# A hybrid decoder step on one core: a new order of the mixer's work, and two more engines run in order of emission

## The chip, the cores and the metric

The kernel runs on one core of one Trainium2 chip. The metric is the device time of one execution in microseconds (us). TensorE (PE, with its weight loads shown apart as PEld), VectorE (DVE), ScalarE (ACT), GpSimd (POOL) and SyncE (SP, which issues transfers) each work through their own list of instructions and wait for each other by semaphores.

## What is computed

Two layers of a decoder, for a prompt of 256 tokens and 8 samples of 4 new tokens, carried together as 288 columns of a transposed activation. Each layer is: x + half a SwiGLU FFN, then a mixer with three parallel branches, then another half FFN.

```python
def _trunk(x, pos, ret_s, hg_s, lru_h, conv_buf, p):
    for l in range(DEPTH):
        x = x + 0.5 * _swiglu(_rmsnorm(x, p['ffn1_norm'][l]), p['ffn1_w_gate'][l], p['ffn1_w_up'][l], p['ffn1_w_down'][l])
        m, st = _mixer(_rmsnorm(x, p['mix_norm'][l]), pos, l, ret_s[l], hg_s[l], lru_h[l], conv_buf[l], p)
        x = x + m.astype(x.dtype)
        x = x + 0.5 * _swiglu(_rmsnorm(x, p['ffn2_norm'][l]), p['ffn2_w_gate'][l], p['ffn2_w_up'][l], p['ffn2_w_down'][l])
```

The mixer projects the normed input by one wide matrix into queries, keys, values and gates, runs 4 retention heads (width 128 by 256), 8 HGRN2 heads (128 by 128) and an RG-LRU over 8 blocks of 128 channels (convolution, two sigmoid gates, a scan), norms and gates each branch, projects it, and merges the three by sigmoid gates. The new states of all heads are outputs too. d_model is 1024, the FFN's hidden width 2816.

## The kernel before, in words

**Units.** Every large matrix product is cut into units: one unit multiplies a 1024-row, 128-column piece of weights with the activations into a 128 by 288 block. The kernel works in fp32 accuracy with the faster fp32r format: weights are split into a high part `wh` (a copy by ACT, line 127 through `act`) and a low part `wl` (a subtraction by DVE, L231), activations likewise (`chunk` pairs), and `gemm` (L245 to L247) issues 8 x 3 = 24 matmuls per unit: high x high, high x low, low x high. A layer has 44 units of gate and up weights and 24 shorter ones of down weights in each FFN, and 128 units in the mixer.

**Weights.** SP loads 512 KB pieces into five buffers `wr`. `next_w` keeps the splits ahead: when unit n begins, the split of unit n + 2 is emitted (`LOOK = 2`); there are three `wh`/`wl` pairs, so that this split waits until the matmuls of unit n - 1 are done.

**Order of the mixer.** `PLAN` is a list of items, written out by hand: `Rn` and `Hn` are the projections of retention head n (four units) and of HGRN2 head n (three), `Xn` is an input block of the RG-LRU, `GLn`, `GHn`, `GRn` are output gates, `T0n` to `T2n` merge gates, `OLn`, `OHn`, `ORn` output projections, `OMn` the last projection. The rest of the work (the heads themselves, the gates and scans of the RG-LRU, the norms) is written as generators. `pump()` is called after almost every unit and runs one step of every generator without weight, and as many steps of heads as a credit allows (`RATE` is added per pump, up to `CAP`). A head is started with a weight, and the active weights may add up to `MAXACT = 2`: an HGRN2 head weighs 1, a retention head 2, so that it runs alone. Where a unit needs a head that is not done, `until` pumps until it is; `do_h` and `do_r` pump until no head is queued. `norm_later` collects the squares of finished heads, and norms four of them at a time (`NORMS`; Ln and Exp on ACT, each with another table than its neighbours).

**Order on the engines.** `tc.manual_schedule(engines={PE})` (L112) makes the order of emission the order of TensorE's instructions. For the other engines the framework's scheduler chooses an order, with `evac()` as a priority for what empties a PSUM bank. An engine then always works through its list in that order.

**Start of a norm.** A unit's matmuls run on activations that are scaled by the gain but not by 1/rms; the rms comes from `norm_rstd` (a matmul with ones, L284, a square root on ACT, a reciprocal on DVE, L279) after the first unit, and results are multiplied by it. In the mixer the first `NXG = 4` units are done so; meanwhile `renorm` (L445, L483) makes properly normed `chunk` pairs for the others.

**RG-LRU.** `lru_scan` handles four blocks at once: one step has eight exponentials and tanhs and four squares on ACT, a later one four square roots, the next ones the scans on DVE.

**States.** `st` has three buffers of 512 KB. A retention head takes two, an HGRN2 head one; POOL's queue loads them, SP's writes them out when the head is done. A head's first step splits the loaded state (`split_s`, ACT `sh`, DVE `sl`).

**Constants.** The tables for masks and rotary angles are loaded through POOL's queue as the program begins. `derived` (three steps on ACT, with another table each) computes gate constants during the first FFN.

Of the kernel before, what the change touches and what calls it, by code (L numbers as in the profile page):

```python
# [19 lines left out]
P = 128  # L20
# [16 lines left out]
LS = 3 + TP  # L37

WB = 12
NORMS = 4  # L40
LRU = (range(0, 4), range(4, 8))
MAXACT = 2
RATE = 1.65
CAP = 2.5
LOOK = 2
NRAW = 5
HEAD = 4
NXG = 4
EVAC = 100
DOWN = ((0, 8), (8, 15), (15, 22))  # L50
LEVELS = (1, 2, 4, 8, 16, 32, 64)
# [8 lines left out]


PLAN = (
# [4 lines left out]
).split()  # L67


def units_of(item):  # L70
    kind, n = item[:-1], int(item[-1])
    if kind == "H":
        return [("in", C_FH + n), ("in", C_QH + n), ("in", C_IH + n)]
    if kind == "R":
        return [("in", C_QR + n), ("in", C_KR + n), ("in", C_VR + 2 * n), ("in", C_VR + 2 * n + 1)]
    base = {"X": C_XL, "GL": C_GL, "GH": C_GH, "GR": C_GR,
            "T0": C_GATE, "T1": C_GATE + 8, "T2": C_GATE + 16}
    if kind in base:
        return [("in", base[kind] + n)]
    return [({"OL": "lru", "OH": "hgrn", "OR": "ret", "OM": "mix"}[kind], n)]  # L80
# [21 lines left out]
def tile_hybrid(ctx: ExitStack, tc, i, o):  # L102
# [6 lines left out]
    pacc = ctx.enter_context(tc.tile_pool(name="pacc", bufs=3, space=PSUM))  # L109
    pmix = ctx.enter_context(tc.tile_pool(name="pmix", bufs=5, space=PSUM))  # L110

    ctx.enter_context(tc.manual_schedule(engines={mybir.EngineType.PE}))  # L112

    sets = {AF.Sigmoid: 2, AF.Sqrt: 3, AF.Exp: 0, AF.Ln: 5, AF.Silu: 18, AF.Gelu_apprx_tanh: 11, AF.Tanh: 0}
    groups = {"set": None, "cur": [], "prev": []}
# [41 lines left out]
    par = cp.tile([P, NPAR], F32, name="par")  # L157

    scratch = cp.tile([P, 1], F32, name="scratch")

    def ready(func):
        act(scratch, onec, func)
# [2 lines left out]

    def const(name, shape, dt=F32):
        t = cp.tile(list(shape), dt, name="c_" + name)
        nc.gpsimd.dma_start(t, i[name])
        consts[name] = t
        return t  # L170

    ones = cp.tile([P, P], F32, name="ones")
    nc.vector.memset(ones, 1.0)
# [143 lines left out]
    def ffn(l, which, nx, next_norm):  # L317
        xh, xl, ss = nx
        hh, hl = chunks(F32R, NF), chunks(F32R, NF)
        for m in range(NF):  # L320
            pg, pu = accps(), accps()
            for u, ps in ((0, pg), (1, pu)):
                wh, wl = next_w()
                gemm(ps[:, :T], wh, wl, NC, xh, xl, 0, True, True)
                if m == 0 and u == 0:
                    rstd = norm_rstd(ss)
            with evac():
                zg = small([P, T], tag="z", bufs=4)
                tt(zg, pg[:, :T], rstd, ALU.mult)  # L329
                act(zg, zg, AF.Silu)  # L330
                zu = small([P, T], tag="z", bufs=4)
                tt(zu, pu[:, :T], rstd, ALU.mult)  # L332
                tt(zu, zu, zg, ALU.mult)  # L333
                hi, lo = hh[m], hl[m]
                act(hi, zu, AF.Copy)
                tt(lo, zu, hi.bitcast(F32), ALU.subtract)
            pump()
        ny = next_norm()
        ready(AF.Sqrt)
        for m in range(NC):  # L340
            ps = accps()
            for k0, k1 in DOWN:
                wh, wl = next_w()
                for kk in range(k0, k1):
                    a, b, j = hh[kk], hl[kk], kk - k0
                    mm(ps[:, :T], wh[:, j, :], a, start=kk == 0, stop=False)  # L346
                    mm(ps[:, :T], wh[:, j, :], b, start=False, stop=False)  # L347
                    mm(ps[:, :T], wl[:, j, :], a, start=False, stop=kk == NF - 1)  # L348
            with evac():
                stt(x[:, m, :], ps[:, :T], 0.5, x[:, m, :], op0=ALU.mult, op1=ALU.add)  # L350
                next_post(m, ny)
            pump()
        return ny
# [2 lines left out]
    active, queue, done = [], [], set()  # L356

    def start(gen, weight):
        if weight:
            queue.append([gen, weight])  # L360
        else:
            active.append([gen, 0])

    credit = [0.0]

# [17 lines left out]

    def norm_later(sq, scale, scaled):
        later.append((sq, scale, scaled))
        if len(later) == NORMS:
            norms_now()

    def norms_now():
        if later:  # L390
# [37 lines left out]
    def mixer(l, nx):  # L428
# [58 lines left out]

        xx, xcw, xc, rr, ii, aa = {}, {}, {}, {}, {}, {}
        h0 = small([P, NC, NB], tag="h0", bufs=1)
        nc.gpsimd.dma_start(h0, i["state_lru"][l])  # L490
        cv0 = small([P, NC, NB, 3], tag="cv0", bufs=1)
        nc.gpsimd.dma_start(cv0, i["state_conv"][l])
        cr = small([P, T], tag="cr", bufs=1)
        sr = small([P, T], tag="sr", bufs=1)
        nc.gpsimd.dma_start(cr, i["cosc"])
        nc.gpsimd.dma_start(sr, i["sinc"])
        cvo = small([P, NC, 1 + NB, 3], tag="cvo", bufs=1)
        def lru_in(n):
            xx[n], xcw[n], rr[n], ii[n] = chunks(F32, 4, LP)
            xc[n], aa[n], rr[n], ii[n] = (a[:, :LY] for a in (xcw[n], xx[n], rr[n], ii[n]))  # L500
            xn, xcn = xx[n], xc[n]
            xs = seqs(xn[:, LS:])
            lw = small([P, 2, P], tag="lw")
            nc.gpsimd.dma_start(lw, i["lru_w"][l, n])
            nc.gpsimd.memset(xn[:, 0:3], 0.0)
            nc.gpsimd.tensor_copy(xs[:, :, 0:3], cv0[:, n])
            ps = unit_in(C_XL + n)
            psv = ps[:, TP:].rearrange("p (b t) -> p b t", t=DS)
            with evac():
                if normed():  # L510
                    act(xn[:, 3 : 3 + P], ps[:, :P], AF.Copy)
                    act(xn[:, 3 + P : LS], ps[:, P:TP][:, ::-1], AF.Copy)
                    act(xs[:, :, 3:7], psv, AF.Copy)
                else:
                    tt(xn[:, 3 : 3 + P], ps[:, :P], src["r"][:, :P], ALU.mult)
                    tt(xn[:, 3 + P : LS], ps[:, P:TP][:, ::-1], src["r"][:, P:TP][:, ::-1], ALU.mult)
                    tt(xs[:, :, 3:7], psv, src["r"][:, TP:].rearrange("p (b t) -> p b t", t=DS), ALU.mult)
            nc.gpsimd.tensor_copy(cvo[:, n, 0, :], xn[:, TP:LS])
            nc.gpsimd.tensor_copy(cvo[:, n, 1:, :], xs[:, :, 4:7])
            cw = PARAMS["conv_w", l]  # L520
            act(xcn, xn[:, 0:LY], AF.Identity, scale=par[:, cw + n : cw + n + 1], bias=pcol("conv_b", l, n))
            for t in range(1, 4):
                stt(xcn, xn[:, t : t + LY], par[:, cw + 8 * t + n : cw + 8 * t + n + 1], xcn,
                    op0=ALU.mult, op1=ALU.add)
            start(lru_gates(n, lw), weight=0)
            pump()
# [99 lines left out]
        def pairs(a, off, d):  # L626
            return free(a, TP + off, (DS, NB), (1, DS - d))

        def hgrn_head(h, f, k, q, qt, zv, zr):
            st = small([P, NB, P], tag="st", bufs=3)  # L630
            nc.gpsimd.dma_start(st, i["state_hgrn"][l, h])
            pr = small([P, PR], tag="pr", bufs=2)
            tt(pr[:, :T], k, q, ALU.mult)
            lev = []
# [27 lines left out]
            for d in range(1, DS):  # L662
                w = NB * (DS - d)
                po = PR_S[d]
                tt(pr[:, po : po + w].rearrange("p (b t) -> p b t", b=NB), pairs(k, 0, d), pairs(qt, d, d), ALU.mult)
                tt(pairs(qt, d, d), pairs(qt, d, d), pairs(f, 0, d), ALU.mult)
            kc = scale(0)
            qm = sample_q(qt[:, TP:])
            sp = split_s(st)
# [170 lines left out]
        def ret_head(h, q, k, kr, vv, v1):  # L840
            sts = []
            for j in range(2):
                st = small([P, NB, P], tag="st", bufs=3)
                nc.gpsimd.dma_start(st, i["state_ret"][l, h, j])
                sts.append(st)
            dm = small([P, 3 * P], tag="dm", bufs=1)
            nc.gpsimd.dma_start(dm, i["dmask"][h])
            qd = small([P, TS], tag="qd")
            tt(qd, q[:, TP:], qdec[:, h, :], ALU.mult)
            qm = sample_q(qd)  # L850
# [73 lines left out]
        def do_r(h):  # L924
            q = rotary(C_QR + h)
            pump()
            k = rotary(C_KR + h)
            kr = replicate(k)
            pump()
            while queue:  # L930
                pump()
            vv = [vtiles() for _ in range(2)]
            v1 = small([96, 2, P], F32R, tag="v1r", bufs=2)
            for j in range(2):
                zv = zsb(C_VR + 2 * h + j)
                zr = replicate(zv)
                start(ret_v(zv, zr, *vv[j], v1[:, j, :]), weight=0)
                pump()
            start(ret_head(h, q, k, kr, vv, v1), weight=2)

        def ret_v(zv, zr, vT, vs, v1):
            yield
# [55 lines left out]

        run["X"] = do_x
        for item in PLAN:  # L1000
            run[item[:-1]](int(item[-1]))
            if item[0] not in "HRX":
                pump()
# [146 lines left out]
```

## Time and profile before

| | |
|---|---|
| median of 3 runs | 1921.11 us (1916.91 to 1921.69) |
| the profiled execution, its own time | 1919.22 us |
| its span, first to last instruction | 1917.1 us |
| TensorE busy | 97% of the span |
| VectorE, ScalarE busy | 71%, 57% |
| table loads on ScalarE | 86, 110.3 us in all |
| layer 1: FFN, mixer, FFN | from 5.7, from 227.3, from 755.6 us |
| layer 2: FFN, mixer, FFN | from about 965, from 1173.8, from 1702 us |

The span is the time of the instructions; the run's own time is 2.1 us longer, and stands 0.1% below the median. A busy time counts overlapping instructions once; matmuls are pipelined, so that a matmul's own duration (about 0.3 us) is more than twice the distance between two.

### The profile page before, as it was taken

The numbers are of one execution on the slowest core, as the hardware profiler recorded it, in microseconds if no ns is written. First come the engines' busy times: TensorE is split into PE (matmuls) and PEld (weight loads), VectorE is DVE, ScalarE is ACT, GpSimd is POOL, SyncE is SP. The second block draws the span as 40 slices with busy tenths as digits, with TensorE's granted clock in tenths as the row PEclk, the third lists the DMA queues.
The fourth block names the chain that finished last, engine by engine and source line by source line (L and its number), as shares of the span: only waits on it lengthen the run. The fifth ranks groups of instructions, "written<-read, shape, count | busy, mean of one in ns | idle before, by whom it ended". The sixth has DMA issues, their size and how long they took to land.

```text
span 1917.1 us, 36198 instructions
## 1 busy us (share of the span) xinstructions
PE 1860.3 (97%) x14040; PEld 1832.0 (96%) x14040; DVE 1363.4 (71%) x2756; ACT 1098.2 (57%) x2005; POOL 96.0 (5%) x252
## 2 busy tenths in 40 slices
PE   7999999999999989999999999999999999999998
PEld 7999989999899989999999999999999999999997
DVE  6665688877788767665566657888877986676654
ACT  6444478656666665444444444886657656654443
POOL 2000013100000000000000000220000000000000
PEclk9999999999999999999999999999999999999999
DMA  7555545545555555555555554556455554455553
GB/s 248 174 170 159 164 129 181 174 159 187 185 185 157 158 163 163 169 168 157 174 165 167 163 169 141 153 162 213 146 187 183 162 169 139 150 165 166 165 161 95
DMA packets 94843, 318.41 MB, mean 166 GB/s; under 512 B 11248, under 2 KB 17312, under 8 KB 94672
## 3 DMA queue, kind: packets, MB, share of 16 engines
q1 hardware_dynamic: 87552, 293.74, 50.0%
q0 software_dynamic: 6544, 21.77, 3.4%
q8 instruction: 111, 1.82, 0.4%
q10 hardware_dynamic: 576, 0.59, 0.1%
q14 instruction: 60, 0.49, 0.1%
HBM read 295.71 MB, written 20.35 MB: 165 GB/s over the span
## 4 chain that ended last, share of the span: by engine, by line
PE 83%; DVE 8%; ACT 6%; issue 2%; DMA 1%; SPq 0%; POOL 0%; DVEq 0%; POOLq 0%; ACTq 0%
PE acc L245 20%; PE acc L246 20%; PE acc L247 20%; PE acc L347 5%; PE acc L346 5%; PE acc L348 5%; DVE wl L231 2%; ACT chunk L127 2%; ACT wh L127 1%; ACT L127 1%; PE mix L709 1%; DMA st<-in_state_ret 1%; PE mix L609 1%; PE mix L610 1%; DVE sl L208 1%
## 5 line engine op out<-in xcount | busy, mean ns | idle before, releaser
L245 PE MATMUL acc<-chunk,wh 128*128 128x288 f32 x3456 | 1042.6, 302 | 9.7 <-ACT wh L127 7.3
L247 PE MATMUL acc<-chunk,wl 128*128 128x288 f32 x3456 | 1023.2, 296 | 6.0 <-DVE wl L231 6.0
L246 PE MATMUL acc<-chunk,wh 128*128 128x288 f32 x3456 | 1023.9, 296 | 0.2
L127 ACT ACTIVATE wh<-wr 128x1024 fp32r<-128x1024 f32 (+2 forms) x531 | 552.9, 1042 | 671.0 <-PE acc L246 304.4
L231 DVE TENSOR_TENSOR wl<-wr,wh 128x1024 fp32r<-128x1024 f32 (+2 forms) x531 | 637.7, 1201 | 238.8 <-ACT wh L127 236.4
L245 PEld LDWEIGHTS acc<-chunk,wh 128*128 128x128 f32 x3456 | 655.9, 190 | 14.0 <-ACT wh L127 7.6
L247 PEld LDWEIGHTS acc<-chunk,wl 128*128 128x128 f32 x3456 | 655.2, 190 | 7.2 <-DVE wl L231 6.9
L246 PEld LDWEIGHTS acc<-chunk,wh 128*128 128x128 f32 x3456 | 655.9, 190 | 4.8 <-issue 2.4
L346 PE MATMUL acc<-chunk,wh 128*128 128x288 f32 x704 | 206.9, 294 | 0.0
L347 PE MATMUL acc<-chunk,wh 128*128 128x288 f32 x704 | 206.9, 294 | 0.0
L348 PE MATMUL acc<-chunk,wl 128*128 128x288 f32 x704 | 206.9, 294 | 0.0
L348 PEld LDWEIGHTS acc<-chunk,wl 128*128 128x128 f32 x704 | 132.1, 188 | 0.0
L346 PEld LDWEIGHTS acc<-chunk,wh 128*128 128x128 f32 x704 | 132.1, 188 | 0.0
L347 PEld LDWEIGHTS acc<-chunk,wh 128*128 128x128 f32 x704 | 132.1, 188 | 0.0
L127 ACT ACT_TABLE_LOAD x86 | 110.3, 1283 | 2.2 <-PEq L1139 0.8
L332 DVE TENSOR_TENSOR z<-acc,rstd 128x288 f32<-128x288 f32 x88 | 40.2, 457 | 76.5 <-PE acc L247 76.5
L329 DVE TENSOR_TENSOR z<-acc,rstd 128x288 f32<-128x288 f32 x88 | 40.2, 457 | 45.2 <-PE acc L247 45.1
L127 ACT ACTIVATE chunk<-z 128x288 fp32r<-128x288 f32 x120 | 52.9, 442 | 17.4 <-DVE z L955 10.3
L208 DVE TENSOR_TENSOR sl<-st,sh 128x512 fp32r<-128x512 f32 x64 | 42.8, 686 | 6.8 <-ACT sh L127 6.2
L333 DVE TENSOR_TENSOR z<-z,z 128x288 f32<-128x288 f32 x88 | 40.3, 458 | 10.1 <-ACT z L127 1.4
L127 ACT ACTIVATE kc<-w 128x128 f32<-128x128 f32 x96 | 29.7, 310 | 28.2 <-DVE w L648 14.3
L647 DVE TENSOR_TENSOR w<-w,w 128x128 f32<-128x128 f32 x112 | 34.1, 304 | 12.5 <-PE mix L709 12.5
(207 smaller groups left out, 1729.1 us busy)
## 6 DMA issues: line engine op xcount, KB each, us to landing
wr<-in_wmx SPq DMA_DIRECT2D x256, 512.0 KB, 3.7
wr<-in_wgu SPq DMA_DIRECT2D x175, 512.0 KB, 3.6
wr<-in_wd SPq DMA_DIRECT2D x64, 448.0 KB, 3.3
wr<-in_wd SPq DMA_DIRECT2D x32, 512.0 KB, 3.5
st<-in_state_ret POOLq DMA_DIRECT2D x16, 512.0 KB, 5.2
st<-in_state_hgrn POOLq DMA_DIRECT2D x16, 512.0 KB, 6.1
out_ret_s<-st SPq DMA_DIRECT2D x16, 512.0 KB, 4.2
out_hgrn_s<-st SPq DMA_DIRECT2D x16, 512.0 KB, 2.8
```

The lines of the kernel that those rows point to most:

```text
L127: r = nc.scalar.activation(out, src, func, **kw)
L208: tt(lo, raw, hi.bitcast(F32), ALU.subtract)
L231: tt(wl[:, k, :], rv, wh[:, k, :].bitcast(F32), ALU.subtract)
L245: mm(ps, wh[:, k, :], xh[k0 + k], start=st, stop=False)
L246: mm(ps, wh[:, k, :], xl[k0 + k], start=False, stop=False)
L247: mm(ps, wl[:, k, :], xh[k0 + k], start=False, stop=sp)
L329: tt(zg, pg[:, :T], rstd, ALU.mult)
L332: tt(zu, pu[:, :T], rstd, ALU.mult)
L333: tt(zu, zu, zg, ALU.mult)
L346: mm(ps[:, :T], wh[:, j, :], a, start=kk == 0, stop=False)
L347: mm(ps[:, :T], wh[:, j, :], b, start=False, stop=False)
L348: mm(ps[:, :T], wl[:, j, :], a, start=False, stop=kk == NF - 1)
```

## The change

The mixer's `PLAN` is another order of the same units, with items `N` that norm all heads collected so far (`NORMS` is gone). A retention head weighs 1, so that two heads of any kind run side by side, and a head whose weight fits is started at once. `RATE` is 1.4 in place of 1.65. An HGRN2 head's first step is cut in two by a further `yield`, ahead of its state split. `NXG` is 8. DVE and ACT are added to the engines that run in order of emission. The first norm of the program is emitted after the second unit in place of the first. All of POOL's loads wait until a copy of the fifth FFN block (`m == HOLD`) is made, and constants are loaded then.

```diff
-NORMS = 4
-RATE = 1.65
+RATE = 1.4
+HOLD = 4
-NXG = 4
+NXG = 8
...
 PLAN = (
-    "R0 T20 X0 X1 X2 X3 H0 X4 X5 T21 X6 T22 T23 X7 T24 R1 GL0 H1 GL1 GL2 GL3 GL4 GL5 T25 T26 T27 H2 GL6 "
...
+    "R0 X0 H0 X1 X2 T20 X3 X4 T21 X5 T22 R1 X6 T23 X7 H1 GL0 GL1 GL2 GL3 R2 T24 T25 GL4 GL5 GL6 GL7 N H2 "
+    "T26 T27 OL0 OL1 R3 OL2 OL3 OL4 OL5 H3 OL6 OL7 GR0 GR1 N H4 GR2 GR3 GR4 T00 GH0 H5 T01 T02 GR5 T03 N "
...
-    ctx.enter_context(tc.manual_schedule(engines={mybir.EngineType.PE}))
+    ctx.enter_context(tc.manual_schedule(engines={mybir.EngineType.PE, mybir.EngineType.DVE, mybir.EngineType.Activation}))
...
+    gate = []
+
+    def pdma(out, src):
+        r = nc.gpsimd.dma_start(out, src)
+        tc.add_manual_dep(r.ins, gate[0].name, mybir.DependencyInfo(
+            mybir.DependencyClass.NoSync, mybir.DependencyReason.DATA), reason="after the start")
+
+    def load_consts():
+        for name, t in consts.items():
+            pdma(t, i[name])
...
-                if m == 0 and u == 0:
+                if m == 0 and u == first:
                     rstd = norm_rstd(ss)
...
+            if first and m == HOLD:
+                gate.append(nc.gpsimd.tensor_copy(scratch2, hh[m][:, :1].bitcast(F32)).ins)
+                load_consts()
...
     def start(gen, weight):
-        if weight:
+        if weight and (queue or sum(a[1] for a in active) + weight > MAXACT):
             queue.append([gen, weight])
         else:
-            active.append([gen, 0])
+            active.append([gen, weight])
...
     def norm_later(sq, scale, scaled):
         later.append((sq, scale, scaled))
-        if len(later) == NORMS:
-            norms_now()
...
+            yield
             kc = scale(0)
             qm = sample_q(qt[:, TP:])
             sp = split_s(st)
...
-            start(ret_head(h, q, k, kr, vv, v1), weight=2)
+            start(ret_head(h, q, k, kr, vv, v1), weight=1)
...
         for item in PLAN:
+            if item == "N":
+                norms_now()
+                continue
```

What moves on the engines is shown at two places of the first mixer. The first is DVE just after the mixer's first unit, where the norm's reciprocal is made. Names: `rstd` is 1/rms, `z` a unit's result times it, `cr`/`sr` the rotary angles, `w` and `chunk` in L445 and L483 (L460 and L498 in the changed file) the renormed activations, `wl` the low part of a coming unit's weights. Before:

```order
L231 TENSOR_TENSOR wl_2629<-wr_2454,wh_2628 128x1024
L279 RECIPROCAL rstd_2603<-rstd_2603 128x288
L469 TENSOR_TENSOR z_2606<-acc_2576,rstd_2603 128x288
L469 TENSOR_TENSOR z_2657<-acc_2632,rstd_2603 128x288
L834 TENSOR_TENSOR w_2608<-z_2606,cr_2564 128x288
L835 TENSOR_TENSOR w_2609<-z_2606,sr_2565 64x288
L836 TENSOR_TENSOR w_2609<-z_2606,sr_2565 64x288
L445 SCALAR_TENSOR_TENSOR w_2614<-x,par,rstd_2603 128x288
L837 TENSOR_TENSOR w_2608<-w_2608,w_2609 128x288
L445 SCALAR_TENSOR_TENSOR w_2618<-x,par,rstd_2603 128x288
```

With the change, from the result of the first unit on:

```order
L484 TENSOR_TENSOR z_2608<-acc_2578,rstd_2605 128x288
L850 TENSOR_TENSOR w_2610<-z_2608,cr_2566 128x288
L851 TENSOR_TENSOR w_2611<-z_2608,sr_2567 64x288
L852 TENSOR_TENSOR w_2611<-z_2608,sr_2567 64x288
L853 TENSOR_TENSOR w_2610<-w_2610,w_2611 128x288
L460 SCALAR_TENSOR_TENSOR w_2616<-x,par,rstd_2605 128x288
L498 TENSOR_TENSOR chunk_2554<-w_2616,chunk_2546 128x288
L460 SCALAR_TENSOR_TENSOR w_2620<-x,par,rstd_2605 128x288
L498 TENSOR_TENSOR chunk_2555<-w_2620,chunk_2547 128x288
L460 SCALAR_TENSOR_TENSOR w_2624<-x,par,rstd_2605 128x288
L498 TENSOR_TENSOR chunk_2556<-w_2624,chunk_2548 128x288
L244 TENSOR_TENSOR wl_2631<-wr_2456,wh_2630 128x1024
```

The fourth unit's `wl` stood ahead of the reciprocal; now it stands behind it, the first unit's rotary and three rounds of the renorm. In each round DVE makes `w`, ACT copies it into the high `chunk`, and DVE subtracts that copy; before, the rounds overlapped one another, now each is finished before the next begins.

The second place is ACT in the first group of the RG-LRU scan (`lru_scan`), between two weight splits. Before (the eight exponentials and tanhs write `chunk` with `par`, 128x312; `so` is a head's state on its way out, `z` and `zrep` a value projection):

```order
L127 ACT_TABLE_LOAD
L127 ACTIVATE chunk_2831<-chunk_2833,par_103 128x312
L127 ACTIVATE so_3213<-mix_3205 128x128
L127 ACTIVATE so_3216<-mix_3205 128x128
L127 ACTIVATE chunk_2833<-chunk_2833,par_103 128x312
L127 ACTIVATE chunk_2887<-chunk_2889,par_103 128x312
L127 ACTIVATE chunk_2960<-chunk_2962,par_103 128x312
L127 ACTIVATE z_3252<-acc_3227 128x288
L127 ACTIVATE chunk_2889<-chunk_2889,par_103 128x312
L127 ACTIVATE zrep_3254<-z_3252 128x96
L127 ACTIVATE chunk_2962<-chunk_2962,par_103 128x312
```

With the change, the end of the same group, up to the next split:

```order
L129 ACTIVATE chunk_3239<-chunk_3239,par_96 128x312
L129 ACTIVATE chunk_2773<-chunk_2772 128x312
L129 ACTIVATE chunk_3021<-chunk_3020 128x312
L129 ACTIVATE chunk_3090<-chunk_3089 128x312
L129 ACTIVATE chunk_3238<-chunk_3237 128x312
L129 ACT_TABLE_LOAD
L129 ACTIVATE chunk_3328<-mix_3491,par 128x312
L129 ACTIVATE chunk_3329<-mix_3494,par 128x312
L129 ACTIVATE kc_3525<-w_2882 128x128
L129 ACTIVATE os_3528<-mix_3505 64x128
L129 ACTIVATE wh_3534<-wr_3245 128x1024
```

Before, the results of other units and heads were emptied between the exponentials. With the change the group stands as one block: four instructions of the evacuation and convolution of one unit, a table load, eight exponentials and tanhs, four squares, a second table load, two gate sigmoids and two small copies, and only then the next `wh`. Over the whole program ACT has 108 table loads with the change.

## Rows read from the trace of the kernel before

**Rows 1.** The page's part 1: busy time, share of the span, instructions.

```profile
PE 1860.3 (97%) x14040; PEld 1832.0 (96%) x14040; DVE 1363.4 (71%) x2756; ACT 1098.2 (57%) x2005; POOL 96.0 (5%) x252
```

**Rows 2.** Busy time by stretch: from:to, length, then PE, PEld, DVE, ACT, POOL, clock.

```profile
227.30:371.40 144.10, 136.41 (x1009) 131.12 (x1008) 121.07 (x265) 105.52 (x236) 29.01 (x83) 0.98 0.51 155
371.40:755.60 384.20, 373.20 (x2845) 365.80 (x2844) 292.51 (x728) 242.17 (x490) 16.17 (x35) 0.99 0.54 171
755.60:1173.80 418.20, 418.20 (x3171) 417.65 (x3170) 260.89 (x360) 193.04 (x264) 1.04 (x2) 1.00 0.56 167
1173.80:1316.20 142.40, 134.88 (x1009) 129.54 (x1008) 121.95 (x269) 105.78 (x236) 25.80 (x79) 0.99 0.50 154
1316.20:1702.00 385.80, 376.20 (x2876) 368.67 (x2875) 299.01 (x744) 245.34 (x494) 11.46 (x25) 0.99 0.53 167
```

**Rows 3.** Waits of PE over the whole span: us in total, times, longest.

```profile
PE mix L398 <- ACT w L127: 7.6, 2, 3.8
...
PE mix L886 <- ACT os L127: 7.1, 4, 3.4
PE acc L247 <- DVE wl L231: 6.0, 4, 2.5
...
PE mix L581 <- ACT zrep L127: 2.4, 2, 1.2
```

**Rows 4.** Timeline of PE at the start: start us, us, instruction, idle before it.

```profile
18.62 1.33 PE L284 MATMUL mix<-ss,ones 128*128 128x288 f32 x2 [4.42 <-DVE ss L270]
...
25.09 0.29 PE L245 MATMUL acc<-chunk,wh 128*128 128x288 f32 x1
```

**Rows 5.** Two short stretches, columns as in the second group; the clock is what matters.

```profile
19.00:22.00 3.00, 3.00 (x12) 2.71 (x12) 2.22 (x2) 2.57 (x3) 0.00 (x0) 0.50 1.03 393
246.00:250.00 4.00, 4.00 (x21) 3.98 (x20) 3.94 (x8) 1.08 (x3) 0.00 (x0) 0.57 0.57 162
```

**Rows 6.** POOL's transfer queue in the first 30 us: packets, MB, share of 16 engines.

```profile
q0 software_dynamic: 1072, 2.93, 27.4%
```

**Rows 7.** ACT in the first FFN, the last step of `derived`.

```profile
40.53 0.21 ACT L127 ACTIVATE par<-par 128x16 f32<-128x16 f32 x1
```

**Rows 8.** The page's groups of weight splits and table loads: busy us, mean ns.

```profile
L127 ACT ACTIVATE wh<-wr 128x1024 fp32r<-128x1024 f32 (+2 forms) x531 | 552.9, 1042 | 671.0 <-PE acc L246 304.4
L231 DVE TENSOR_TENSOR wl<-wr,wh 128x1024 fp32r<-128x1024 f32 (+2 forms) x531 | 637.7, 1201 | 238.8 <-ACT wh L127 236.4
...
L127 ACT ACT_TABLE_LOAD x86 | 110.3, 1283 | 2.2 <-PEq L1139 0.8
```

**Rows 9.** Timeline of DVE and ACT at the first mixer's start.

```profile
232.91 1.95 DVE L279 RECIPROCAL rstd<-rstd 128x288 f32<-128x288 f32 x1
...
234.90 0.82 DVE L469 TENSOR_TENSOR z<-acc,rstd 128x288 f32<-128x288 f32 x2
...
237.04 0.52 DVE L445 SCALAR_TENSOR_TENSOR w<-x,par,rstd 128x288 f32<-128x288 f32 x1
...
237.60 0.45 ACT L127 ACTIVATE chunk<-w 128x288 fp32r<-128x288 f32 x1 [2.11 <-DVE w L445]
...
238.65 0.45 DVE L483 TENSOR_TENSOR chunk<-w,chunk 128x288 fp32r<-128x288 f32 x1
```

**Rows 10.** Timeline of ACT around the scans of the first mixer.

```profile
277.73 1.06 ACT L127 ACTIVATE wh<-wr 128x1024 fp32r<-128x1024 f32 x1 [2.39 <-PE acc L246]
...
287.40 1.07 ACT L127 ACTIVATE wh<-wr 128x1024 fp32r<-128x1024 f32 x1
...
323.51 3.24 ACT L127 ACTIVATE chunk<-chunk,par 128x312 f32<-128x312 f32 x7
...
327.27 1.16 ACT L127 ACTIVATE chunk<-chunk 128x312 f32<-128x312 f32 x3
```

**Rows 11.** The chain that ended last, where a head waits for its state: start, us, what.

```profile
485.17 4.39 DMA out_ret_s<-st
490.14 6.34 DMA st<-in_state_ret
```

More of the change, by code (lines that the diff above doesn't have):

```diff
@@ L62 @@
 PLAN = (
[4 rows of a table removed]
[4 rows of a table added]
 ).split()
 def units_of(item):
+    if item == "N":
+        return []
     kind, n = item[:-1], int(item[-1])
@@ L159, in tile_hybrid @@
     scratch = cp.tile([P, 1], F32, name="scratch")
+    scratch2 = cp.tile([P, 1], F32, name="scratch2")
     def ready(func):
@@ L167, in const @@
         t = cp.tile(list(shape), dt, name="c_" + name)
-        nc.gpsimd.dma_start(t, i[name])
         consts[name] = t
         return t
+    gate = []
[6 more added lines that the diff above has]
+            pdma(t, i[name])
     ones = cp.tile([P, P], F32, name="ones")
@@ L319, in ffn @@
         hh, hl = chunks(F32R, NF), chunks(F32R, NF)
+        first = int(l == 0 and which == 1)
         for m in range(NF):
@@ L489, in mixer @@
         h0 = small([P, NC, NB], tag="h0", bufs=1)
-        nc.gpsimd.dma_start(h0, i["state_lru"][l])
+        pdma(h0, i["state_lru"][l])
         cv0 = small([P, NC, NB, 3], tag="cv0", bufs=1)
-        nc.gpsimd.dma_start(cv0, i["state_conv"][l])
+        pdma(cv0, i["state_conv"][l])
         cr = small([P, T], tag="cr", bufs=1)
         sr = small([P, T], tag="sr", bufs=1)
-        nc.gpsimd.dma_start(cr, i["cosc"])
-        nc.gpsimd.dma_start(sr, i["sinc"])
+        pdma(cr, i["cosc"])
+        pdma(sr, i["sinc"])
         cvo = small([P, NC, 1 + NB, 3], tag="cvo", bufs=1)
@@ L503, in lru_in @@
             lw = small([P, 2, P], tag="lw")
-            nc.gpsimd.dma_start(lw, i["lru_w"][l, n])
+            pdma(lw, i["lru_w"][l, n])
             nc.gpsimd.memset(xn[:, 0:3], 0.0)
@@ L630, in hgrn_head @@
             st = small([P, NB, P], tag="st", bufs=3)
-            nc.gpsimd.dma_start(st, i["state_hgrn"][l, h])
+            pdma(st, i["state_hgrn"][l, h])
             pr = small([P, PR], tag="pr", bufs=2)
@@ L843, in ret_head @@
                 st = small([P, NB, P], tag="st", bufs=3)
-                nc.gpsimd.dma_start(st, i["state_ret"][l, h, j])
+                pdma(st, i["state_ret"][l, h, j])
                 sts.append(st)
             dm = small([P, 3 * P], tag="dm", bufs=1)
-            nc.gpsimd.dma_start(dm, i["dmask"][h])
+            pdma(dm, i["dmask"][h])
             qd = small([P, TS], tag="qd")
@@ L1000, in mixer @@
         for item in PLAN:
+            if item == "N":
+                norms_now()
+                continue
             run[item[:-1]](int(item[-1]))
```

5 rows, old and new, of the table PLAN are left out of this document.

## The prediction

> **What bounds the kernel now.** I read the page's busy times first: TensorE is busy for 1860.3 of 1917.1 us [rows 1], so all idle time together is 56.8 us, and no order of the work can win more than that and the stretches at half clock. The busy times by stretch show where it lies. In the FFN between the mixers PE is busy for all 418.2 us with 3171 matmuls [rows 2]: 0.132 us each, 3.17 us for a unit of 24. Nothing waits there, so the FFNs have nothing to gain. Each mixer has two parts. In its first 32 units PE idles 7.7 and 7.5 us (144.1 - 136.4, 142.4 - 134.9), with DVE busy for 84% and ACT for 73% of the first; in the other 96 it idles 11.0 and 9.6 us, with DVE at 76% and ACT at 63% [rows 2]. The list of PE's waits names what is late: a norm's square, a sample output `os`, a weight's low part, a copy for a transpose [rows 3]. None is a transfer and none a shortage of an engine over a whole mixer; they are chains in one head that has nothing beside it. A second cost hides in the clock: just after the waits at 240 to 245 us, the stretch from 246 to 250 us ran at a granted 0.57 [rows 5], so 1.7 us more.
>
> The profiled execution took 1919.22 us, 0.1% below the median of 1921.11; sums are made against it. About 0.3%, 5.8 us, is what a measurement of this kernel can tell from no change.
>
> **The start: -8 us.** The norm's matmul stood idle for 4.42 us and ran at 18.62; the second unit followed at a granted 0.50, and the third began at 25.09 [rows 4, 5]. With the change the second unit goes ahead of the norm and fills the wait: first unit done at 14.2 (18.62 - 4.42), second 3.2 us, or nearly twice that at half clock, norm 0.7 (half of the 1.33 that it took at half clock [rows 4]), third at 18.1 to 20.7. POOL's loads, 27.4% of the transfer engines' time in the first 30 us [rows 6], leave the way of the first weights and of x; I take 2 us for that, so 16 to 19, and 17 as the value, since PE no longer pauses. Ends: a gain of 4.4 and of 9.4.
>
> **`derived`: +2.2 us.** Its three table loads (3 x 1.28 [rows 8]) and four small steps (0.21 each [rows 7]) take 4.7 us on ACT. In order of emission they stand between an FFN block's last copy, some 1.5 us after its matmuls, and the next split (1.04 + 1.20 [rows 8]): 8.5 us, against two units, 6.3. Ends 0 and 3.
>
> **The first units of a mixer: +3.8 each.** Where the low part of the fourth unit now stands, the list of DVE in the section on the change tells; its time is a sum. From the first unit's end: norm 0.7, square root 0.45 (as the ACT copy), reciprocal 1.95, the result 0.41 (two in 0.82), rotary 4 x 0.41, then three rounds of 0.52 + 0.45 + 0.45 with 0.1 between engines, 4.5, then the low part, 1.20 [rows 4, 8, 9]: 10.9, and 11.6 with the other handovers. Two units and the norm cover 7.1: 4.5 late. The fifth unit's low part follows 8.5 later (the same from the result on, with a split on ACT behind the last copy), its cover is 3.2: 5.3 late. Together 9.5 with a small rest for the sixth. Before, the waits here were 1.2 and 2.5 (the longest of their kinds in [rows 3]) and the half clock 1.7 [rows 5]: 5.7. Ends 0 and 6. `NXG = 8` doesn't help: it moves the first use of the renormed chunks, not the splits.
>
> **The scans: +8 in each mixer.** With the change ACT has one block between two splits: eight at 3.24/7, four at 1.16/3 [rows 10], two table loads, and eight others at 0.31, the mean of ACT without splits and loads ((1098.2 - 552.9 - 110.3)/1388 [rows 1, 8]): 3.7 + 1.5 + 2.6 + 2.5 = 10.3, then the split, 2.2. It may begin only when the unit two back is done, since that unit's evacuation stands ahead of it. The cover is two units with their small matmuls, 2 x 4.0 (136.4 + 373.2 us busy in the first mixer, over 128 units [rows 2]), and the small ones before: 8.5. So 4 late, twice in a mixer, a little less for the square roots that follow at two more loads. Before, such a block lasted as long, 277.73 to 287.40 between two splits [rows 10], and cost PE nothing, since later units' work was emptied inside it. So the ends are 0 and 10.
>
> Here a rule of the Trainium skill bears. The rows show a load of 1283 ns [rows 8] with the next instruction right behind it. The page ScalarE: Activation LUTs (What ACT_TABLE_LOAD costs) adds a drain of about 1.38 us to each switch of set, which no row of this trace shows. By it the eight loads that lie in and just behind the two blocks would make this term 19 us instead of 8, an estimate from that page; I keep the measured 1.28.
>
> **A state that comes late: +4 in each mixer.** The third retention head takes the two state buffers of the second, which ends only two units before it. Write-out and load took 4.39 and 6.34 us [rows 11], with some 3 us until the last update 14; its split on ACT comes up after two units of 4.0 and an evacuation, 9.5. Everything behind it on ACT waits, the weight splits too, where before only the head waited. Some of the 4.5 is covered. Ends 0 and 6.
>
> **No slack in the first third: +6 in each mixer.** Counted with the durations of these rows, less the tenth by which neighbours overlap, DVE has 125 us of work among units 3 to 32 in the new order, against 126 us of TensorE; in the old it was 117 against 124. An engine in strict order at 99% loses PE's time with every wait for ACT. Ends 0 and 16.
>
> **What is won: -18 over both mixers.** The 11.0 and 9.6 us of late idle time [rows 2], 3.7 in each first part beyond its start's 4, and the half clock (0.02 x 144 + 0.01 x 912 by the clock column, 12, less the starts' 3.4) would all go at best: 36. The new order has a second head beside every head, no item that must pump until something is done, and norms placed well ahead of their users, so the waits for `w` and `os` go. But ACT gets 11 more table loads a mixer (14 us), and with DVE at four fifths and more of PE's time a strict order makes new waits: a norm's silu, product, copy and subtraction run back and forth between ACT and DVE. I take half. Ends 8 and 36.
>
> Sum: -8 + 2.2 + 2 x (3.8 + 8 + 4 + 6) - 18 = +19.8, so 1919.2 + 19.8 = **1939 us**. The rest lies beside other work: the FFNs' evacuations in order end about 2 us after a unit, with 6.3 us until their split is needed; the later loads of constants meet a transfer share of about half [rows 2]; the six DVE instructions and three ACT ones that are moved by `yield` cost nothing by themselves.
>
> **Rivals.** *Faster, 1895.* The point that decides is whether the work between an evacuation and the next low part stays under the 7 to 8.5 us that two units cover. If lag of one block is made good in the next, as ACT's 73% and DVE's 84% in the first part allow on average, then the scans, the late state and the lack of slack cost nothing, and two thirds of the possible gain come: -8 + 2.2 + 7.6 - 26 = -24. For it speaks that the old scan blocks of 9.7 us cost nothing and that every long wait in the list is one that a second head covers. Against it speak the two places shown, where the sum on DVE or ACT is 11 to 12.5 us. *No change, 1919.* The scans and the first units cost what I say, but state and slack nothing: -8 + 2.2 + 23.6 - 18 = 0.
>
> **How the numbers follow.** Slower, as forecast, 0.55: the two sums for the first units and the scans rest on fixed lists and measured durations, and already eat the gain of the start and half of the rest. Faster 0.33, even 0.12. The forecast's own range is 1925 to 1968: the upper ends of the four costs add 32 (2 x 16.2) and hardly come all together, so 29; the lower end is where it would still be slower than before. For 8 in 10 the range must reach past the faster rival: 1888 to 1968.
>
> **What would show it.** Right: PE's idle time falls after the first third and rises in it; DVE's share in the first 32 units is above 85% and PE waits there for `wl` most of all; the fourth unit begins some 4 us late; between two `wh` in the scans ACT is busy for 10 us without a pause, and PE waits behind it; the third unit of the program begins near 17 us. Wrong: `wl` waits of under 2 us in all in the first third, or PE's idle time in the mixers below 20 us.

## The result, and the profile after

The changed kernel takes **2040.35 us** (median of 4 runs, 2039.62 to 2042.42) against 1921.40 in the same comparison: a ratio of 1.0625, 95% interval 1.0608 to 1.0642. It is slower, as forecast, but by 119 us instead of 20, far outside the range. The profiled execution took 2039.97 us, its span is 2038.1.

The page's busy times, which answer to [rows 1]:

```profile
PE 1900.9 (93%) x14040; PEld 1857.0 (91%) x14040; DVE 1388.7 (68%) x2768; ACT 1131.4 (56%) x2019; POOL 84.8 (4%) x253
```

The same 14040 matmuls are busy for 40.6 us more, and TensorE idles 137.2 us instead of 56.8 (+80.4). Together that is the 121 us of span. The mean granted clock over the span is 0.976 after and 0.990 before, so 48.9 and 19.2 us lost (2038.1 x 0.024, 1917.1 x 0.010): at most 30 of the 40.6 us is clock. What makes the rest is not shown. VectorE and ScalarE have only 25 and 33 us more to do. In the chain of work that ended last, TensorE's share of the span falls from 83% to 61%; VectorE's rises from 8% to 18%, ScalarE's from 6% to 16%.

Busy time in the first mixer, units 0 to 31 and units 32 to 119, columns as in [rows 2] (whose second stretch ends at a later unit); the second mixer is alike, 181.1 and 375.3 us:

```profile
225.40:404.90 179.50, 150.16 (x1018) 142.36 (x1017) 129.54 (x286) 107.74 (x234) 23.28 (x83) 0.90 0.39 121
404.90:778.50 373.60, 348.19 (x2637) 336.88 (x2638) 272.56 (x678) 240.24 (x471) 16.03 (x35) 1.00 0.53 165
```

The first 32 units went from 144 to 180 us, and VectorE's share there fell, 84% to 72%: the engine did not run out of time, it stood. TensorE's part of that is 21.6 us more idle (29.3 against 7.7) and 13.8 us more busy at a clock of 0.90 in place of 0.98. The longest waits of TensorE, as in [rows 3]:

```profile
PE mix L725 <- ACT kc L129: 43.6, 27, 4.2
PE acc L258 <- ACT wh L129: 20.2, 8, 6.3
PE acc L260 <- DVE wl L244: 12.0, 22, 1.7
PE mix L742 <- DVE w L668: 9.4, 6, 3.1
PE acc L258 <- ACT chunk L129: 9.2, 6, 2.1
PE mix L926 <- ACT chunk L129: 9.1, 2, 4.6
PE mix L902 <- ACT os L129: 6.3, 2, 3.2
```

The first is new. Before, it was:

```profile
PE mix L709 <- ACT kc L127: 1.7, 2, 0.9
```

An HGRN2 head's matmul waits for a copy that its own previous step made. One such wait, on VectorE, ScalarE and TensorE in turn (start, duration, instruction, idle before it and what ended it):

```profile
565.81 0.46 DVE L498 TENSOR_TENSOR chunk<-z,chunk 128x288 fp32r<-128x288 f32 x1 [0.51 <-ACT chunk L129]
566.18 0.39 DVE L662 TENSOR_TENSOR w<-w,w 128x128 f32<-128x128 f32 x1
...
567.38 0.19 DVE L613 TENSOR_TENSOR qm<-w,qm 128x32 fp32r<-128x32 f32 x1 [0.45 <-ACT qm L129]
567.90 1.29 DVE L221 TENSOR_TENSOR sl<-st,sh 128x512 fp32r<-128x512 f32 x2 [0.33 <-ACT sh L129]
...
569.94 1.22 DVE L244 TENSOR_TENSOR wl<-wr,wh 128x1024 fp32r<-128x1024 f32 x1
571.08 0.28 DVE L662 TENSOR_TENSOR w<-w,w 128x128 f32<-128x128 f32 x1
...
571.66 0.31 ACT L129 ACTIVATE kc<-w 128x128 f32<-128x128 f32 x1 [0.51 <-DVE w L668]
...
564.52 0.38 PE L725 MATMUL mix<-w,kc 128*128 128x128 f32 x2
...
572.02 0.49 PE L725 MATMUL mix<-w,kc 128*128 128x128 f32 x2 [2.85 <-ACT kc L129]
```

The head's matmul ran at 564.52, so its next scaling (L662, at 571.08) could have begun at 564.9. In VectorE's row there stand before it an evacuation, a whole step of the other head (566.18 to 570.0) and the low part of a weight, three of them waiting for ScalarE. `kc` then takes one more hand-off, and TensorE has only one unit of matmuls to cover it all.

### The profile page after: what moved, and what is told of

The parts are those of the page before. It is cut to its first block, busy times and chain, and to the rows that moved or that the text cites. A ratio compares the mean times of both kernels' runs of the same rounds, so it can differ in the third digit from the quotient of the medians.

```text
span 2038.1 us, 36036 instructions
## 1 busy us (share of the span) xinstructions
PE 1900.9 (93%) x14040; PEld 1857.0 (91%) x14040; DVE 1388.7 (68%) x2768; ACT 1131.4 (56%) x2019; POOL 84.8 (4%) x253
## 4 chain that ended last, share of the span: by engine, by line
PE 61%; DVE 18%; ACT 16%; issue 4%; DMA 1%; POOL 0%; SPq 0%; DVEq 0%; ACTq 0%; POOLq 0%
PE acc L260 14%; PE acc L258 14%; PE acc L259 14%; DVE wl L244 6%; ACT wh L129 5%; PE acc L365 5%; PE acc L364 5%; PE acc L363 5%; ACT L129 3%; ACT chunk L129 3%; ACT w L129 1%; DVE w L662 1%; ACT kc L129 1%; ACT sh L129 1%; DVE w L663 1%
## 5 line engine op out<-in xcount | busy, mean ns | idle before, releaser
L258 PEld LDWEIGHTS acc<-chunk,wh 128*128 128x128 f32 x3456 | 665.5, 193 | 36.9 <-ACT wh L129 22.2
L260 PEld LDWEIGHTS acc<-chunk,wl 128*128 128x128 f32 x3456 | 664.3, 192 | 19.0 <-DVE wl L244 18.8
L259 PEld LDWEIGHTS acc<-chunk,wh 128*128 128x128 f32 x3456 | 665.5, 193 | 6.0 <-issue 2.4
L129 ACT ACTIVATE wh<-wr 128x1024 fp32r<-128x1024 f32 (+2 forms) x531 | 546.3, 1033 | 115.7 <-ACT wh L129 63.4
L365 PEld LDWEIGHTS acc<-chunk,wl 128*128 128x128 f32 x704 | 132.1, 188 | 1.0 <-DVE wl L244 1.0
L363 PEld LDWEIGHTS acc<-chunk,wh 128*128 128x128 f32 x704 | 132.1, 188 | 0.0
L364 PEld LDWEIGHTS acc<-chunk,wh 128*128 128x128 f32 x704 | 132.1, 188 | 0.0
L129 ACT ACTIVATE z<-z 128x288 f32<-128x288 f32 x88 | 39.1, 445 | 146.0 <-DVE z L343 146.0
L725 PE MATMUL mix<-w,kc 128*128 128x128 f32 x192 | 41.1, 296 | 43.7 <-ACT kc L129 43.6
L350 DVE TENSOR_TENSOR chunk<-z,chunk 128x288 fp32r<-128x288 f32 x88 | 40.3, 458 | 54.6 <-ACT chunk L129 54.6
L725 PEld LDWEIGHTS mix<-w,kc 128*128 128x128 f32 x192 | 30.7, 192 | 51.0 <-ACT kc L129 50.1
L129 ACT ACTIVATE chunk<-x,par 128x288 fp32r<-128x288 f32 x48 | 25.3, 534 | 84.6 <-DVE x L367 58.0
```

Source lines behind the costliest of these rows:

```text
L129: r = nc.scalar.activation(out, src, func, **kw)
L258: mm(ps, wh[:, k, :], xh[k0 + k], start=st, stop=False)
L259: mm(ps, wh[:, k, :], xl[k0 + k], start=False, stop=False)
L260: mm(ps, wl[:, k, :], xh[k0 + k], start=False, stop=sp)
L725: mm(pl, kc, lev[li][4], start=True, stop=True)
```

## The experiments

All kernels keep the whole computation. us is the median; the ratio is to the kernel before, run beside each. The kernel before has medians from 1915.9 to 1921.4 us in these comparisons, so differences of us between kernels of different comparisons are good to some 5 us. In the table, "units 0-31" and "units 32-119" are the lengths of these units in both mixers together (spans of the profiled execution), "tails" the two stretches behind, to the next mixer and to the end.

| kernel | us | ratio (95%) | to mixer 1 | units 0-31 | units 32-119 | tails |
|---|---|---|---|---|---|---|
| before | 1916 to 1921 | 1 | 227.3 | 286.4 | 714.2 | 689.2 |
| the change | 2040.4 | 1.0625 (1.0608, 1.0642) | 225.3 | 360.7 | 748.9 | 703.2 |
| start_only | 1910.5 | 0.9957 (0.9942, 0.9972) | 221.1 | 286.5 | 709.8 | 689.3 |
| plan_only | 1927.4 | 1.0048 (1.0029, 1.0066) | 221.1 | 292.4 | 719.8 | 689.3 |
| act_only | 1929.4 | 1.0051 (1.0031, 1.0072) | 226.6 | 319.2 | 693.0 | 689.2 |
| dve_only | 2003.6 | 1.0442 (1.0424, 1.0460) | 227.0 | 328.4 | 759.1 | 688.4 |
| kc_vector | 1995.1 | 1.0412 (1.0392, 1.0433) | 225.7 | 344.8 | 718.0 | 704.8 |
| kc_lo | 1974.3 | 1.0278 (1.0264, 1.0292) | 227.2 | 330.7 | 711.6 | 703.2 |

### Which engine's order costs

```diff
-    ctx.enter_context(tc.manual_schedule(engines={mybir.EngineType.PE, mybir.EngineType.DVE, mybir.EngineType.Activation}))
+    ctx.enter_context(tc.manual_schedule(engines={mybir.EngineType.PE}))
```

This is plan_only; dve_only and act_only leave DVE or Activation beside PE in the set. start_only is the kernel before with `first`, `HOLD`, `gate` and `pdma` as in the change.

> The change with TensorE alone in emission order; the scheduler orders VectorE and ScalarE again; plan, pace, two heads, start and renorm block stay. Order theory (the strict order makes VectorE and ScalarE wait for one another, and TensorE for both): 1900 to 1930 us, the first 32 units of each mixer near 144 us again, waits for kc of 43.6 us gone to under 10. Plan theory (two heads always under way put each head's steps too close to their copies, whatever the order): 1990 us or more, the kc waits stay at 25 us or more.

> The change with TensorE and VectorE in emission order, ScalarE ordered by the scheduler. Order theory, with VectorE as the engine that carries most of the loss (scale and evacuation wait in its row): 1980 to 2020 us. With ScalarE as that engine: 1915 to 1950 us, waits for kc under 15 us. Plan theory: 1990 us or more, as with the plan alone.

> The change with TensorE and ScalarE in emission order, VectorE ordered by the scheduler. Order theory, with ScalarE as the engine that carries most of the loss (kc, wh and the os copies that TensorE waited for are all its instructions): 1980 to 2020 us. With VectorE as that engine: 1915 to 1950 us. If the loss needs both rows, both single-engine kernels lie under 1960 us and their losses do not add up to 119 us.

> The kernel before with only the start of the change: first norm behind the second unit, loads on GpSimd's queue held until the fifth pair of units. If the 8 us won at the third unit (25.09 to 17.14 us) last to the end: 1911 to 1915 us. If they are given back at the next late place (the derived constants, the loads held back): 1919 to 1923 us.

The strict order costs 113 us (2040.4 - 1927.4; 111 by the ratios); the plan theory falls, though the waits for `kc` in plan_only fell to 13.6 us and not under 10. Over the whole run VectorE's order alone costs 76, ScalarE's alone 2, ScalarE's on top of VectorE's 37. By stretch the 2 is a balance: against plan_only, ScalarE's order costs 27 us in units 0 to 31 and gives back 27 in units 32 to 119, where VectorE's costs 36 and 39; both together cost 68 and 29. So in the first 32 units each of the two orders costs, and behind them VectorE's does. The list of waits names ScalarE's instructions instead. The waits for `kc` come with VectorE's row (dve_only first, then act_only):

```profile
PE mix L725 <- ACT kc L129: 43.6, 28, 3.3
```

```profile
PE mix L725 <- ACT kc L129: 5.5, 8, 1.4
```

Of VectorE's and ScalarE's waits, summed over all rows of each list: VectorE stood 300 us for ScalarE before, 321 in plan_only, 361 in act_only, 513 in dve_only and 541 after; ScalarE for VectorE 116, 103, 505, 273 and 694. 505 us of ScalarE standing cost 2 us in sum while the scheduler ordered VectorE's row; in these five kernels it is VectorE's standing that goes with the time (not in all: in wl_late, below, it is 540 us as in the change, and the time is 52 us longer). The start is won: 6.5 us, kept to the end. But the plan with the scheduler costs 17 against start_only; forecast was that it wins.

### Whose cover is too short

look3 has the weights' cover raised from two units to three; the raw buffers go down from five to three:

```diff
-LOOK = 2
-NRAW = 5
+LOOK = 3
+NRAW = 3
...
-    wrp = ctx.enter_context(tc.tile_pool(name="wrp", bufs=5))
-    wsp = ctx.enter_context(tc.tile_pool(name="wsp", bufs=3))
+    wrp = ctx.enter_context(tc.tile_pool(name="wrp", bufs=3))
+    wsp = ctx.enter_context(tc.tile_pool(name="wsp", bufs=4))
```

> The change with the weights split three units ahead instead of two (four split buffers, three raw ones). Weights theory, on which the prediction's terms rested (late work comes through the two-unit cover of wh and wl): waits for wh and wl together fall from 32 us to under 10 us, 1985 to 2015 us. Step theory (a head's own next matmul has one unit of cover whatever the weights do): kc waits stay at 35 us or more, 2020 to 2045 us.

2040.7 us, ratio 1.0645 (1.0624 to 1.0666). The waits for weights went (32.2 us for `wh` and `wl` in the change, 7.1 here), and the same time came back at `kc` and at a value's transpose:

```profile
PE mix L725 <- ACT kc L129: 61.4, 26, 9.4
PE mix L595 <- DVE z L484: 20.1, 2, 10.1
...
PE acc L258 <- ACT wh L129: 6.4, 1, 6.4
```

So a longer cover for the weights buys nothing here. The first units show how: the fourth unit begins 10.0 us after the first in place of 13.5, and the fifth at 23.9 as in the change (23.7). kc_vector takes out one hand-off between the strict rows:

```diff
-                    act(kc.rearrange("p (n c j) -> p n c j", c=2, j=hw), kv, AF.Copy)
+                    nc.vector.tensor_copy(kc.rearrange("p (n c j) -> p n c j", c=2, j=hw), kv)
```

> The change with each head's copy kc made by VectorE, right behind the scaling that it copies, instead of by ScalarE: one hand-off less between a step and the head's next matmul, and some 0.3 us more on VectorE for each copy. Hand-off theory (kc is late because it crosses from one strict row to another): waits of TensorE for kc fall under 15 us, 1985 to 2020 us. Load theory (VectorE's own row is what is too long): 2045 us or more.

1995.1 us, ratio 1.0412 (1.0392 to 1.0433): 45 us (41 by the ratios) from 96 small copies moved to the fuller engine. Of this 31 are won in units 32 to 119, which are back at plan_only's length (718.0 against 719.8), and 16 in units 0 to 31, which stay 52 above it. The wait left:

```profile
PE mix L725 <- DVE kc L673: 22.4, 19, 2.7
```

It did not fall under 15, but the load theory, which wanted a slower kernel, falls. late_lo takes out another hand-off; a low half is put in a list and issued at the end of `pump` (so also in `put_y`):

```diff
                 act(hi, zu, AF.Copy)
-                tt(lo, zu, hi.bitcast(F32), ALU.subtract)
+                lows.append((lo, zu, hi.bitcast(F32)))
```

> The change, all three engines in emission order, with the low halves of each feed-forward and mixer activation (a VectorE subtraction that waits for ScalarE's copy just ahead of it) issued behind the unit's step instead of ahead of it; same work. Head-of-line theory (in the strict row VectorE stands idle for ScalarE's copy, 54.6 us at L350 and 40.9 us at L498, and the steps behind it are late by that much): those two waits fall under 20 us together, 1990 to 2020 us. Weights theory (what is late are the splits, two units ahead, and they stand where they stood): 2030 to 2050 us.

2019.9 us, ratio 1.0539 (1.0515 to 1.0563), 20 us won (16 by the ratios), yet the 95.5 us of waits that were to vanish are still 64.4: most moved behind the step with the instruction. kc_lo has both edits.

> The change with both edits that helped: kc copied by VectorE, and the activations' low halves behind the unit's step. Hand-off theory (each hand-off between the two strict rows that leaves the stretch between a step and the next one shortens it): the gains add, 1970 to 1982 us. If both took out the same idle time: 1988 to 1996 us, as with kc alone.

1974.3 us, ratio 1.0278 (1.0264 to 1.0292): 45 + 20 = 65 forecast by adding, 66 measured (by the ratios 41 + 16 = 57, and 67). They are two idle times, not one. Of the strict order's 113 us, 47 are still there; by span 38 in units 0 to 31, 14 in the tails and 6 before mixer 1, less 8 in units 32 to 119. No run takes these apart by hand-off; they go when the scheduler orders the rows.

### Two that made it worse

wl_late issues the low half of a mixer weight one unit later (`wls` is emptied at the head of the next `next_w`), late_both does that and late_lo:

```diff
-            tt(wl[:, k, :], rv, wh[:, k, :].bitcast(F32), ALU.subtract)
+            if FF <= (pos["split"] - 1) % (2 * FF + len(ORDER)) < FF + len(ORDER):
+                wls.append((wl, raw, wh, k, step))
+            else:
+                tt(wl[:, k, :], rv, wh[:, k, :].bitcast(F32), ALU.subtract)
```

> The change with the low half of each mixer weight (VectorE's subtraction, which waits for ScalarE's copy of the high half) issued one unit later, behind the evacuation and the step of a unit instead of ahead of them; high halves and the feed-forward parts as they are. Head-of-line theory (VectorE's strict row stands idle for ScalarE's copies, here 111.6 us in the two mixers' units 0 to 119, and everything behind is late): those waits fall under 30 us and the time to 1975 to 2015 us. Rival (the low half now has one unit of cover, and TensorE waits for it instead): waits of TensorE for wl over 40 us, 2040 to 2080 us.

> Both of these: the mixer weights' low halves one unit later, and the activations' low halves behind the unit's step. Head-of-line theory with gains that add: 20 us under the run with the weights' low halves alone, 1955 to 1995 us. If the first of the two already removes the idling that matters: within 8 us of the better of the two single runs.

2092.8 us (ratio 1.0919, 1.0893 to 1.0945) and 2064.0 (1.0782, 1.0752 to 1.0812). The rival was right in kind, too low in time (2040 to 2080), and late_both missed both of its ranges. The wait changes place, from the head's copy to the weight:

```profile
PE acc L270 <- DVE wl L253: 132.8, 74, 7.0
...
PE mix L735 <- ACT kc L130: 4.8, 2, 2.4
```

So one unit of cover is too little for a weight's low half. Whether `kc` is in time here because VectorE comes to it sooner, or because TensorE comes later, is not shown.

steps_first issues a unit's step behind the next unit's matmuls and ahead of that unit's evacuation (`settle` runs the step that `turn`, in the place of `pump`, has owed):

```diff
             gemm(ps[:, :T], wh, wl, NC, a, b, 0, True, True)
+            settle()
             return ps[:, :T]
```

> The change with each mixer unit's pump step issued right behind the next unit's matmuls, ahead of that unit's evacuation instead of behind the previous one; same work, still strict. If kc is late because evacuations stand between a step's scaling and its copy: kc waits fall from 43.6 us to under 20 us, 1980 to 2015 us. If only the total of work and hand-offs per unit on VectorE and ScalarE counts, whatever their order inside a unit: 2030 to 2050 us, kc waits replaced by waits for evacuations.

2107.0 us, ratio 1.0988 (1.0968 to 1.1009): a miss for both expectations.

```profile
PE mix L742 <- ACT kc L129: 84.8, 25, 6.4
```

What it did to the rows: VectorE and ScalarE stood for the steps' small matmuls 74 us in all (11.5 + 62.7), in the change 23 (0.7 + 22.0). An evacuation ahead of a step seems to give TensorE the time to run the step's matmuls; that accounts for 51 of the 67 us only if each of them counts, and was not tried by itself.

### The tails, the plan, and a version that is faster

ffn_strict has the scheduler in units 0 to 119 of the mixers and strict order elsewhere; act_region has TensorE alone, and ScalarE beside it from unit 34 to 120, by leaving and entering the guard between items of `PLAN`. For act_region:

```diff
         for item in PLAN:
+            if units == 34:
+                in_order(mybir.EngineType.Activation)
+            if units == 120:
+                in_order()
+            units += len(units_of(item))
```

> The change with VectorE and ScalarE in emission order only outside units 0 to 119 of the mixers, that is in the feed-forward parts, the last eight units of a mixer and the start; the scheduler orders them in units 0 to 119. If the 4 us of the start and the 7 us behind each mixer are prices of the strict order in these parts themselves: 1940 to 1950 us (some 18 over the plan alone). If they are late work carried over from the mixers' units: 1925 to 1932 us.

> The change with TensorE alone in emission order, except that ScalarE joins it from the 35th unit of each mixer to the 120th. With VectorE strict being the loss and ScalarE strict a gain there (346.5 us for units 32 to 119 with ScalarE strict, 358.9 with the plan alone): 1898 to 1908 us, which would beat the kernel before and the start alone. If the gain there was paid for by its slow first units (work that had been put off): 1920 to 1930 us.

ffn_strict: 1935.3 us, ratio 1.0102 (1.0080 to 1.0124), between the two forecasts. Of the 18 us that the change loses to plan_only before mixer 1 and in the tails, 5.8 are there (2.8 + 3.0); the rest is gone with the mixers' units scheduled. act_region: **1905.4 us**, ratio 0.9939 (0.9924 to 0.9955). Units 32 to 119 take 349.1 and 349.2 us, against 358.9 and 360.9 in plan_only; there some `kc` stood behind a weight split that the scheduler had put first (the first row). The second row has another cause:

```profile
PE mix L725 <- ACT kc L129: 13.6, 6, 3.4
...
PE mix L725 <- ACT wh L129: 5.8, 2, 2.9
```

In it `kc` had long been copied. On ScalarE, VectorE and TensorE in plan_only:

```profile
380.09 0.31 ACT L129 ACTIVATE kc<-w 128x128 f32<-128x128 f32 x1
386.23 1.15 ACT L129 ACTIVATE sh<-st 128x512 fp32r<-128x512 f32 x2 [5.82 <-DMA st<-in_state_ret]
...
388.10 0.28 DVE L662 TENSOR_TENSOR w<-w,w 128x128 f32<-128x128 f32 x1
...
388.53 0.46 PE L725 MATMUL mix<-w,kc 128*128 128x128 f32 x2 [2.92 <-ACT wh L129]
```

ScalarE stood 5.82 us for a retention head's state, VectorE 5.70 us for ScalarE's half of its split, and the HGRN2 head's scaling L662, which makes an operand of the matmul, stood behind that split. This is the prediction's late state, in a kernel where only TensorE's order is strict. In act_region ScalarE stands for this state only 2.5 and 2.6 us, the second row is gone, and the first is 9.8. plan_kc and region_kc are plan_only and act_region with `kc` on VectorE.

> The plan alone (TensorE alone in emission order) with kc copied by VectorE. If the plan's own 17 us over the start alone are the same hand-off (13.6 us of waits for kc and 5.8 at the same line, before the clock): 1908 to 1918 us. If they come from elsewhere in the plan: 1923 to 1932 us.

> The version with ScalarE in emission order from the 35th unit to the 120th of each mixer, and kc copied by VectorE. If the waits for kc that it still has (9.8 us) are what is left to win: 1894 to 1902 us. If VectorE, now busier, pays as much as is won: 1903 to 1910 us.

plan_kc: 1922.8 us, ratio 1.0020 (1.0007 to 1.0032), so some 5 of the plan's 17 us. The expectation took the late state's 5.8 us for the same hand-off; plan_kc still has these waits, 2.4 and 3.3, now put down to VectorE's L662. The rest stays open. region_kc: 1905.4 us, ratio **0.9915** (0.9902 to 0.9929), the lowest ratio of all, below start_only's interval; in us it is level with act_region, so `kc` on VectorE is not shown to help there. The before's plan with ScalarE strict was not tried.

## Why the prediction was wrong

Direction and three places were right, the size was not. The step that failed is the rivals' "the point that decides", on which the terms for the strict order rested: that late work reaches TensorE through weights, with the 7 to 8.5 us that two units cover. look3 refutes it: with three units the time is the same. In units 32 to 119 what decides is the one unit between a head's step and its next matmul, with two rows between that wait for each other; taking one of its hand-offs away was worth 31 us there, where the strict order costs 29, and 45 in all. In units 0 to 31 the strict order costs 34 us a mixer where three terms had 17.8. Their idle time was not far off (21.6 us more than before in the first mixer); that TensorE is also busy for 13.8 us more there, at a clock of 0.90 in place of 0.98, was in none of them. The second large failure is the -18 for the new plan.

The start's rows and those of the first mixer (PE):

```profile
17.14 0.51 PE L258 MATMUL acc<-chunk,wh 128*128 128x288 f32 x1
...
38.88 0.40 PE L258 MATMUL acc<-chunk,wh 128*128 128x288 f32 x1 [1.18 <-ACT wh L129]
40.39 0.40 PE L260 MATMUL acc<-chunk,wl 128*128 128x288 f32 x1 [0.98 <-DVE wl L244]
...
238.87 0.40 PE L258 MATMUL acc<-chunk,wh 128*128 128x288 f32 x1 [3.39 <-ACT wh L129]
240.13 0.61 PE L260 MATMUL acc<-chunk,wl 128*128 128x288 f32 x1 [0.73 <-DVE wl L244]
...
248.68 0.44 PE L595 MATMUL mix<-c_ident,z 128*128 128x128 f32 x2 [2.91 <-DVE z L484]
...
313.03 0.80 PE L926 MATMUL mix<-v1r,km 96*128 96x256 f32 x2 [4.56 <-ACT chunk L129]
```

ScalarE in the first scan block:

```profile
304.20 1.28 ACT L129 ACT_TABLE_LOAD   x1
305.49 4.25 ACT L129 ACTIVATE chunk<-chunk,par 128x312 f32<-128x312 f32 x8
```

- **Start, -8: right.** The third unit began at 17.14 (17 forecast, 25.09 in [rows 4]); 6.2 us of span at mixer 1 in start_only.
- **`derived`, +2.2: half of the cost.** The two waits at 39 and 40 us are 2.16, as forecast, but the clock from 41 to 45 us was 0.57: 1.7 more. The change reached mixer 1 4.2 us behind start_only.
- **First units, +3.8 each: somewhat low.** The fourth unit waited 3.39 + 0.73 (4.5 forecast). The forecast's two terms, 4.5 and 5.3, add to 9.8, not 9.5. Unit 5, counted from 0, began 28.8 us after unit 0, before 22.7: +6.1. The next wait was not a weight but a transpose's copy.
- **Scans, +8 each: right in size.** Behind the first mixer's two blocks TensorE stands 4.56 and 3.2 us, and the clock comes on top. But a head's matmul waits there for what stands at the end of the block (a gate sigmoid for L926, the copy `os` for L902), not for a weight. In the block a load of 1.28 began at 304.20, 0.02 us behind the instruction before it, and the next instruction at 305.49. By the Trainium skill (ScalarE: Activation LUTs, What ACT_TABLE_LOAD costs) a drain of some 1.38 us comes on top of each load; the trace again shows none.
- **Late state, +4 each: not seen in the change.** In units 32 to 119 of the first mixer waits for `wh` and `wl` are 0.5 and 2.8 us in all, and ScalarE stands for a state 0.7 us in the whole run. It is seen in plan_only, 2.9 us a mixer at TensorE.
- **No slack, +6 each: the wrong reason.** VectorE's share fell instead of passing 85%, and the waits for `wl` in the first third, said to be the most, are 2.0 us.
- **What is won, -18: failed.** It was the other large miss: under the scheduler the new plan's mixers are 11.7 us longer than before (1012.2 against 1000.5), 15.9 longer than start_only's. Of this 5.8 us of waits are the late state and some 5 us the copies `kc`; the rest is open.
- **No term at all** for the heads' own steps past the first third (+34.7 us in units 32 to 119 of both mixers, `kc` first in the waits there), for the tails (+14.0), or for the clock behind each new wait.

By parts of span: start -2.0 (forecast -5.8), plan in the mixers +11.7 (-18), strict order in them +97.3 (1109.5 - 1012.2; forecast 43.6), of which 68.3 in units 0 to 31, and tails +14.0 (none); sum 121.0.

## What to carry to other kernels

Before two engines are put in order of emission, list for each consumer on the bound engine not how full they are but the hand-offs between them that stand ahead of its operand, and what of the bound engine's own work covers them: a step that feeds its own next step has the shortest cover. A list of waits names the last releaser; which row is to blame is told by freeing one engine at a time, and read by stretch: over the whole run a loss and a gain of 27 us looked like nothing. And when a longer cover only moves the wait to another name, the whole row, with its own waits, is late, not that operand alone.

## What was not expected of the hardware

A wait goes on costing after it has ended, in clock. Stretches at and behind the scan's wait (length, PE, PEld, DVE, ACT, POOL, granted clock, transfers):

```profile
308.00:313.00 5.00, 0.48 (x4) 0.25 (x2) 1.66 (x4) 4.91 (x11) 0.45 (x4) 0.80 0.00 0
313.00:318.00 5.00, 4.97 (x21) 4.97 (x22) 3.39 (x10) 3.37 (x7) 0.00 (x0) 0.52 0.02 3
```

After 4.56 us of idling the next 5 us ran at a granted 0.52, close to the lower of the two levels (1.2 of 2.4 GHz), another 2.4 us. Over the run TensorE idles 80.4 us more and is busy 40.6 us more with the same matmuls, at most 30 of it by the clock.
